# Hymba decoder block on one Trainium2 core: loading the output projection's operand two token tiles ahead

## The chip, the core and the metric

The kernel runs on one core of a Trainium2 chip. A core has TensorE (PE in the rows; its weight loads are PEld), VectorE (DVE), ScalarE (ACT), GpSimd (POOL) and SyncE (SP), each working through its own instructions in order; here every DMA is issued from SP's queue, also in order. The metric is the device time of one execution in microseconds (us): the median of the runs, lower is better. The kernel before takes 1448.87 us (median of 3 runs, 1448.34 to 1451.42).

## The reference

One layer of a hybrid decoder block, in float32: 1024 tokens and 16 meta tokens ahead of them, model width 1024.

```python
proj = rmsnorm(h, g_attn) @ w_in
# group A: 4 heads of differential attention; group B: 8 heads of stick-breaking attention
o_diff = _rmsnorm(o_diff, g_diff) * (1.0 - lam_init)
o_sb = _rmsnorm(o_sb, g_sb)
merged = jnp.concatenate([heads of o_diff, heads of o_sb], axis=-1)
h = h + merged @ w_out
h = h + (silu(gate) * up) @ w_down      # gate, up: causal convolution of rmsnorm(h, g_ffn) @ w_up
return _rmsnorm(h, g_final)[:, N_META:]
```

The change is in how the third line from the bottom, `merged @ w_out` and its addition to `h`, is fed.

## The kernel before

**The stages.** The program is written as strands (Python generators) that are advanced in turn, and a scheduler then places the instructions on each engine. Attention is done in eight units of 128 features: four heads of group A, then four pairs of group B. The score strand, the weigh strand and the norm strand carry attention. Everything else that PE can do meanwhile is the fill strand: the input projection of the next units, and, beside the last unit, the output projection. `attend` advances the fill strand so that the nanoseconds that it has yielded (`at["fill"]`) keep up with a share of the attention work done. A yield of a function instead of a number is a gate: the fill strand stays there until the function is true.

**The merged features.** For each unit the norm strand normalises a group of query tiles: PE transposes the norm factors (line 669), DVE multiplies (670), ACT and POOL split the result into a high and a low part, the tile `mc` (lines 672 and 673), and SP writes `mc` to `merged` in DRAM (674). The set `merged_at` tells which unit and tile has been written at that point of the program.

**The output projection.** It is done in three parts of the sum over units: OUT_A (units 0 to 2), OUT_B (3 to 5), OUT_C (6 and 7). Token tiles 5 to 8 are the late tiles, 3, 4, 0, 1, 2 the early ones (0 is the meta tile with two rows). The order of visits is OUT_A late, OUT_A early, OUT_B late, OUT_C late, OUT_B early, OUT_C early, in all 27 visits of a part and a tile. For each visit `load_merged` (line 702) fills a tile `mt` from `merged` by two DMAs (line 709; 192 KB each with three units, 128 KB with two), in OUT_A also the residual tile `acc` from `x` (line 711). Then `out_tile` (line 730) does two halves of 512 columns. Each half is 3 matmuls per unit into a bank `mm` of PSUM (line 743), 9 in OUT_A and OUT_B and 6 in OUT_C, and one DVE addition to `acc` (line 745). `out_meta` does the meta tile (lines 721 and 723).

**What sets the order around the change.** `out_part` (line 747) loads the next tile of the same part when it starts a tile, if that tile's features are in `merged_at`. `mt` has two buffers, so that load waits for the tile before the current one. The first tile of each part has no such load ahead of it: it is loaded where its turn comes. The very first load also has to wait until the input projection has read `xT` for the last time, because the pool of `mt` takes over that memory. SP's queue carries, between these loads, the writes of `merged` (line 674), the query swaps `qs` (522, 523), the weights (`raw`, line 684) and, later, the rows `y_rows` of the second norm (877).

After the output projection come the second norm, the feed-forward stages (lines 909 and 1045), and the down projection (1203, 1221).

Of the kernel before, what the change touches and what calls it, by code (L numbers as in the profile page):

```python
# [8 lines left out]
F32 = mybir.dt.float32  # L9
F32R = mybir.dt.float32r  # L10
# [3 lines left out]
ALU = mybir.AluOpType  # L14
# [3 lines left out]
P = 128  # L18
D = 1024
# [30 lines left out]
LATE_TILES = (5, 6, 7, 8)  # L50
EARLY_TILES = (3, 4, 0, 1, 2)
# [12 lines left out]
N_LATE = 12  # L64
AHEAD_OUT = 2
BEHIND = 2

# [28 lines left out]
def hybrid_block(ctx: ExitStack, tc: tile.TileContext, x, meta, g_attn, w_in, lq1, lk1, lq2, lk2,  # L96
                 g_diff, g_sb, w_out, g_ffn, w_up, conv_w, conv_b, w_down, g_final, out):
    nc = tc.nc
# [534 lines left out]
    merged_at = set()  # L633
# [53 lines left out]
    def load_split(src, tag, raw=None):  # L687
        raw = load_raw(src) if raw is None else raw
        bufs = 3 if tag == "wu" else 2
        hi = room[tag].tile([P, D], F32R, tag=tag + "h", name=tag + "h", bufs=bufs)  # L690
        lo = room[tag].tile([P, D], F32R, tag=tag + "l", name=tag + "l", bufs=bufs)
        nc.scalar.copy(hi, raw)
        nc.gpsimd.tensor_tensor(lo, raw, f(hi), op=ALU.subtract)
        return hi, lo
# [4 lines left out]
    def resid(t):  # L699
        return room["accm"][:2] if t == 0 else room["acc"][:, t - 1, :]  # L700

    def load_merged(t, us):
        c, n = q_span(t)
        mt = room["wd"].tile([P, 3, 2, P], F32R, tag="mt", name="mt", bufs=2)
        if t == 0:
# [8 lines left out]
    def out_meta(us, wo, mt):  # L714

        for h in range(2):
# [7 lines left out]
            if us is OUT_C:  # L724
                nc.scalar.copy(room["low"][:, hs], room["accm"][32:34, hs])
                nc.vector.tensor_tensor(resid(0)[:, hs], resid(0)[:, hs], room["low"][:, hs], op=ALU.add)
        if us is OUT_C:
# [7 lines left out]
    def out_tile(t, us, wo, mt):  # L735
# [10 lines left out]
        if us is OUT_C:  # L746
            square_sum(t)

    def out_part(us, wo, ts_):

        nxt = None
        for i, t in enumerate(ts_):
            if nxt is None:
                yield lambda: all((u, t) in merged_at for u in us)
                nxt = load_merged(t, us)
            mt, nxt = nxt, None
            if i + 1 < len(ts_) and all((u, ts_[i + 1]) in merged_at for u in us):
                nxt = load_merged(ts_[i + 1], us)
            yield from out_tile(t, us, wo, mt) if t else out_meta(us, wo, mt)

    def out_strand():
# [11 lines left out]
        room["accm"] = room["wd"].tile([34, D], F32, tag="wdh", name="accm", bufs=2)  # L773
        room["low"] = room["wd"].tile([2, D], F32, tag="wdl", name="low", bufs=2)
        nc.gpsimd.memset(room["accm"], 0.0)
# [415 lines left out]
    k = 0  # L1191
# [79 lines left out]
```

## Time and profile before

| What | us |
|---|---|
| median of 3 runs (lowest to highest) | 1448.87 (1448.34 to 1451.42) |
| the profiled execution | 1450.97 |
| its span, from the first to the last instruction | 1449.2 |
| PE busy in the span | 1359.0 (94%) |
| DVE, ACT, POOL busy | 969.8, 714.1, 745.1 |
| stretch with the output projection's matmuls | 548.5 to 734.0 |

The profiled execution is 2.1 us above the median. Its span leaves 1.8 us for what lies around the instructions. Matmuls are pipelined: a row's duration is longer than the distance from one start to the next, so a stretch is read by its starts, by the idle time in brackets, and by the granted clock, not by the durations alone. The granted clock is a fraction of 2.4 GHz: 1.00 is that level, and 0.51 over a stretch means that nearly all of it ran at the lower level of 1.2 GHz.

### The profile page before, as it was taken

What the parts mean: (1) busy time and instruction counts of PE and PEld (TensorE: products, weight loads), DVE (VectorE), ACT (ScalarE), POOL (GpSimd) and SP (SyncE); (2) the same over time, 40 slices, a digit from 0 to 9 for tenths busy, and PEclk for the clock granted to TensorE, in tenths of its full rate; (3) what the DMA queues carried; (4) which work ended last, traced back from release to release, by engine and by line L of the source; (5) the groups of instructions that cost most, each with busy time, mean ns of one, the idle gap of its engine ahead of it and who ended that gap; (6) DMA issues with size and microseconds to landing.
All of it is one profiled execution on the core that took longest, in us unless ns stands there. A gap on an engine that the chain in (4) does not pass through costs nothing.

```text
span 1449.2 us, 24692 instructions
## 1 busy us (share of the span) xinstructions
PE 1359.0 (94%) x9000; PEld 1259.0 (87%) x9000; DVE 969.8 (67%) x1816; ACT 714.1 (49%) x1406; POOL 745.1 (51%) x769
## 2 busy tenths in 40 slices
PE   5999989999998998898899999999999996999997
PEld 5989989998887796776689899999999995888886
DVE  8377868778676775874577545555556565977755
ACT  6255655666575664541344354445444453533322
POOL 5145444236665765662101376667666672965620
PEclk9999999999999998999999999999999998999999
DMA  5154454221211117333534222322323234966502
GB/s 211 51 179 154 143 166 139 59 67 38 60 44 50 46 46 207 92 90 93 143 109 162 92 70 95 109 93 78 100 96 110 94 104 163 335 206 199 179 15 102
DMA packets 93569, 166.35 MB, mean 115 GB/s; under 512 B 11628, under 2 KB 46060, under 8 KB 93448
## 3 DMA queue, kind: packets, MB, share of 16 engines
q1 hardware_dynamic: 93448, 164.78, 36.3%
q8 instruction: 71, 1.16, 0.3%
q14 instruction: 50, 0.41, 0.1%
HBM read 111.49 MB, written 44.85 MB: 108 GB/s over the span
## 4 chain that ended last, share of the span: by engine, by line
PE 68%; DVE 6%; DMA 4%; issue 3%; ACT 2%; POOL 2%; SPq 0%; DVEq 0%; POOLq 0%; ACTq 0%
PE x L1045 27%; PE ps_mm L296 7%; PE ps_x L1203 7%; PE ps_mm L743 5%; PE ps_y L1203 5%; PE ps_av L587 3%; DMA mt<-merged 3%; PE ps_tr L558 3%; DVE s L500 2%; PE ps_s L909 2%; PE ps_av L909 2%; PE ps_x L1221 2%; PE ps_y L1221 2%; PE ps_s L443 1%; PE ps_s L444 1%
## 5 line engine op out<-in xcount | busy, mean ns | idle before, releaser
L296 PE MATMUL ps_mm<-xT_hi,wh 128*128 128x342 f32 (+7 forms) x552 | 183.5, 333 | 4.8 <-DVE qz L306 3.5
L296 PE MATMUL ps_mm<-xT_lo,wh 128*128 128x342 f32 (+7 forms) x552 | 180.5, 328 | 0.2 <-DVE xT_lo L183 0.2
L296 PE MATMUL ps_mm<-xT_hi,wl 128*128 128x342 f32 (+7 forms) x552 | 179.9, 327 | 0.0
L587 PE MATMUL ps_av<-aT,v 128*128 128x256 f32 (+3 forms) x608 | 132.7, 309 | 3.1 <-POOL aT L565 2.6
L890 POOL TENSOR_TENSOR dl<-raw,dh 128x1024 fp32r<-128x1024 f32 (+1 forms) x43 | 82.1, 1910 | 90.1 <-ACT dh L889 88.5
L1045 PE MATMUL x<-yh,dl 128*128 128x258 f32 x608 | 124.2, 286 | 0.0
L1045 PE MATMUL x<-yl,dh 128*128 128x258 f32 x608 | 123.7, 285 | 0.0
L1045 PE MATMUL x<-yh,dh 128*128 128x258 f32 x608 | 123.7, 285 | 0.0
L296 PEld LDWEIGHTS ps_mm<-xT_hi,wh 128*128 128x128 f32 x552 | 106.1, 193 | 8.0 <-issue 2.6
L500 DVE TENSOR_TENSOR_SCAN s<-s 128x912 f32<-128x912 f32 (+6 forms) x72 | 99.3, 1383 | 20.6 <-POOL s L496 19.5
L558 PE MATMUL ps_tr<-ident,a 128*128 128x128 f32 (+1 forms) x540 | 94.2, 280 | 18.9 <-DVE aT L563 4.7
L1051 ACT COPY kept<-x 128x516 f32<-128x516 f32 x76 | 44.8, 589 | 133.6 <-PE x L1045 133.6
L1173 POOL TENSOR_TENSOR el<-down_raw,eh 128x512 fp32r<-128x512 f32 x53 | 91.3, 1752 | 35.9 <-ACT eh L1171 35.9
L587 PEld LDWEIGHTS ps_av<-aT,v 128*128 128x128 f32 (+2 forms) x608 | 97.1, 193 | 13.4 <-issue 4.4
L296 PEld LDWEIGHTS ps_mm<-xT_lo,wh 128*128 128x128 f32 x552 | 106.3, 193 | 1.1 <-DVE xT_lo L183 0.5
L501 POOL TENSOR_TENSOR a<-a,s 128x912 f32<-128x912 f32 (+3 forms) x64 | 82.1, 1286 | 47.5 <-DVE s L500 40.4
L296 PEld LDWEIGHTS ps_mm<-xT_hi,wl 128*128 128x128 f32 x552 | 106.0, 192 | 0.3
L570 DVE TENSOR_TENSOR aT<-ps_tr,aT 128x512 fp32r<-128x512 f32 (+3 forms) x132 | 76.7, 586 | 42.2 <-ACT aT L569 41.3
L1045 PEld LDWEIGHTS x<-yh,dh 128*128 128x128 f32 x608 | 95.3, 191 | 0.0
L1045 PEld LDWEIGHTS x<-yl,dh 128*128 128x128 f32 x608 | 95.1, 191 | 0.0
L1045 PEld LDWEIGHTS x<-yh,dl 128*128 128x128 f32 x608 | 95.0, 191 | 0.0
L569 ACT CAST aT<-ps_tr 128x512 fp32r<-128x512 f32 (+3 forms) x132 | 66.5, 510 | 56.1 <-PE ps_tr L558 53.2
(306 smaller groups left out, 4074.3 us busy)
## 6 DMA issues: line engine op xcount, KB each, us to landing
raw<-in_w_up SPq DMA_DIRECT2D x44, 512.0 KB, 3.6
down_raw<-blocks SPq DMA_DIRECT2D x63, 256.0 KB, 4.0
raw<-in_w_in SPq DMA_DIRECT2D x24, 512.0 KB, 3.6
blocks<-cg SPq DMA_DIRECT2D x45, 256.0 KB, 2.8
raw<-in_w_down SPq DMA_DIRECT2D x18, 512.0 KB, 3.6
down_sums<-raw SPq DMA_DIRECT2D x18, 512.0 KB, 3.2
down_raw<-down_sums SPq DMA_DIRECT2D x36, 256.0 KB, 4.6
down_raw<-in_w_down SPq DMA_DIRECT2D x27, 256.0 KB, 4.2
```

Source lines behind the costliest of these rows:

```text
L296: nc.tensor.matmul(ps[:, :w], a[:, kt * P : (kt + 1) * P], b[:, kt, c0 : c0 + w], start=(kt == 0 and i == 0), stop=(kt == KT - 1 and i == 2))
L500: nc.vector.tensor_tensor_scan(s[:n, rev], s[:n, rev], s[:n, rev], 1.0, op0=ALU.mult, op1=ALU.bypass)
L501: (nc.gpsimd if t else nc.vector).tensor_tensor(b[:n, :keys], b[:n, :keys], s[:n, 1 : keys + 1], op=ALU.mult)
L558: pe_last[0] = nc.tensor.transpose(ps[:kn, at : at + qn], a[:qn, kk0 : kk0 + kn], ident[:qn, :qn])
L569: nc.scalar.copy(aT[:kn, 0, f0:end], ps[:kn, f0:end])
L570: nc.vector.tensor_tensor(aT[:kn, 1, f0:end], ps[:kn, f0:end], f(aT)[:kn, 0, f0:end], op=ALU.subtract)
L587: pe_last[0] = nc.tensor.matmul(av[:, :w], v[:kn, kt, vi, :], aT[:kn, ai, j * w : (j + 1) * w], start=job["count"] == 0, stop=job["count"] ...
L743: nc.tensor.matmul(ps[:n], a, b[:, hs], start=(j == 0 and i == 0), stop=(j == len(wo) - 1 and i == 2))
L890: nc.gpsimd.tensor_tensor(lo[:, :w], src, f(hi)[:, :w], op=ALU.subtract)
L1045: nc.tensor.matmul(x[:, s], w[a][:, ks], y[b][:, kt, SUB * s : SUB * s + SUB + 2], start=start and kt == 0 and i == 0, stop=kt == KT // 2 ...
L1173: engine.tensor_tensor(lo[:, cs], raw[:, cs], f(hi)[:, cs], op=ALU.subtract)
L1203: nc.tensor.matmul(ps, a[:, P * t : P * (t + 1)], b[:, upper], start=begin and j == 0 and i == 0, stop=j == n - 1 and i == 2, skip_group_c ...
```

## The change

All 27 visits are listed in one table, `visits`, over the ends of the parts. When a visit starts, everything up to two visits further on is loaded, as far as its features are in `merged_at` at that point of the program; `mt` has three buffers. Where a visit's tile has not been loaded when its turn comes, the load is issued there and the fill strand yields LOAD_NS = 4000 ns, so that `attend` counts 4 us of fill work that isn't there and issues attention instead. The tile `low` for the meta row moves into two buffers of the pool tag `mc`, and the low part of one weight has one buffer instead of two.

```diff
--- before.py
+++ after.py
@@ -63,6 +63,7 @@
 S_AHEAD = 2
 N_LATE = 12
 AHEAD_OUT = 2
+LOAD_NS = 4000.0
 BEHIND = 2
 
 
@@ -686,9 +687,9 @@
 
     def load_split(src, tag, raw=None):
         raw = load_raw(src) if raw is None else raw
-        bufs = 3 if tag == "wu" else 2
-        hi = room[tag].tile([P, D], F32R, tag=tag + "h", name=tag + "h", bufs=bufs)
-        lo = room[tag].tile([P, D], F32R, tag=tag + "l", name=tag + "l", bufs=bufs)
+        bufs = {"wu": (3, 3), "wd": (2, 1)}.get(tag, (2, 2))
+        hi = room[tag].tile([P, D], F32R, tag=tag + "h", name=tag + "h", bufs=bufs[0])
+        lo = room[tag].tile([P, D], F32R, tag=tag + "l", name=tag + "l", bufs=bufs[1])
         nc.scalar.copy(hi, raw)
         nc.gpsimd.tensor_tensor(lo, raw, f(hi), op=ALU.subtract)
         return hi, lo
@@ -701,7 +702,7 @@
 
     def load_merged(t, us):
         c, n = q_span(t)
-        mt = room["wd"].tile([P, 3, 2, P], F32R, tag="mt", name="mt", bufs=2)
+        mt = room["wd"].tile([P, 3, 2, P], F32R, tag="mt", name="mt", bufs=3)
         if t == 0:
             nc.gpsimd.memset(f(mt)[:, : len(us), 0, :34], 0.0)
         for s in range(2):
@@ -722,8 +723,9 @@
                 yield 2 * 512 * COL
             nc.vector.tensor_tensor(room["accm"][:, hs], room["accm"][:, hs], ps[:34], op=ALU.add)
             if us is OUT_C:
-                nc.scalar.copy(room["low"][:, hs], room["accm"][32:34, hs])
-                nc.vector.tensor_tensor(resid(0)[:, hs], resid(0)[:, hs], room["low"][:, hs], op=ALU.add)
+                low = pn.tile([P, 2, 258], F32, tag="mc", name="low", bufs=2).rearrange("p a b -> p (a b)")[:2, :512]
+                nc.scalar.copy(low, room["accm"][32:34, hs])
+                nc.vector.tensor_tensor(resid(0)[:, hs], resid(0)[:, hs], low, op=ALU.add)
         if us is OUT_C:
             square_sum(0)
 
@@ -746,17 +748,34 @@
         if us is OUT_C:
             square_sum(t)
 
+    visits = [(us, t) for us, ts_ in ((OUT_A, LATE_TILES + EARLY_TILES), (OUT_B, LATE_TILES), (OUT_C, LATE_TILES),
+                                      (OUT_B, EARLY_TILES), (OUT_C, EARLY_TILES)) for t in ts_]
+    fetched = []
+
+    def there(k):
+        us, t = visits[k]
+        return all((u, t) in merged_at for u in us)
+
+    def fetch_until(k):
+
+        while len(fetched) <= min(k, len(visits) - 1) and there(len(fetched)):
+            us, t = visits[len(fetched)]
+            fetched.append(load_merged(t, us))
+
+    visit = [0]
+
     def out_part(us, wo, ts_):
 
-        nxt = None
-        for i, t in enumerate(ts_):
-            if nxt is None:
-                yield lambda: all((u, t) in merged_at for u in us)
-                nxt = load_merged(t, us)
-            mt, nxt = nxt, None
-            if i + 1 < len(ts_) and all((u, ts_[i + 1]) in merged_at for u in us):
-                nxt = load_merged(ts_[i + 1], us)
-            yield from out_tile(t, us, wo, mt) if t else out_meta(us, wo, mt)
+        for t in ts_:
+            k = visit[0]
+            visit[0] += 1
+            assert visits[k] == (us, t)
+            if k >= len(fetched):
+                yield lambda: there(k)
+                fetch_until(k)
+                yield LOAD_NS
+            fetch_until(k + 2)
+            yield from out_tile(t, us, wo, fetched[k]) if t else out_meta(us, wo, fetched[k])
 
     def out_strand():
         while len(w_ready) < AHEAD_OUT:
@@ -771,7 +790,6 @@
         nc.gpsimd.memset(room["ss"], 1.0)
         wa = w_ready + [load_split(None, "wd", raw)]
         room["accm"] = room["wd"].tile([34, D], F32, tag="wdh", name="accm", bufs=2)
-        room["low"] = room["wd"].tile([2, D], F32, tag="wdl", name="low", bufs=2)
         nc.gpsimd.memset(room["accm"], 0.0)
         yield from out_part(OUT_A, wa, LATE_TILES)
         yield lambda: done["weighed"] >= UNITS - 1
```

**The first load on PE.** PE's order behind the last matmuls on `xT`, where attention of the last units (lines 443, 444, 558, 587) meets the first output tile (line 743). Before:

```order
L444 MATMUL ps_s<-kz,qs 128x400
L443 MATMUL ps_s<-kz,qz 128x264
L444 MATMUL ps_s<-kz,qs 128x264
L558 MATMUL ps_tr<-ident,a 128x128 x4
L587 MATMUL ps_av<-aT,v 128x256
L743 MATMUL ps_mm<-wh,mt 128x512
L743 MATMUL ps_mm<-wl,mt 128x512
L743 MATMUL ps_mm<-wh,mt 128x512 x2
L587 MATMUL ps_av<-aT,v 128x256 x2
```

Now (all lines from 64 on count one higher, those of the projection two):

```order
L588 MATMUL ps_av<-aT,v 128x256 x4
L559 MATMUL ps_tr<-ident,a 16x128 x2
L588 MATMUL ps_av<-aT,v 128x256 x2
L559 MATMUL ps_tr<-ident,a 128x128 x4
L444 MATMUL ps_s<-kz,qz 128x264
L445 MATMUL ps_s<-kz,qs 128x264
L444 MATMUL ps_s<-kz,qz 2x16
L445 MATMUL ps_s<-kz,qs 2x16
L444 MATMUL ps_s<-kz,qz 128x256
L445 MATMUL ps_s<-kz,qs 128x256
L588 MATMUL ps_av<-aT,v 128x256 x4
L745 MATMUL ps_mm<-wh,mt 128x512
```

What stood behind the first matmuls on `mt` (line 587 x2 and on) now stands ahead of them: 27 more matmuls and transposes of attention lie between the last read of `xT` and the first use of `mt`.

**The first loads on SP.** SP's queue from the first load on; `mt_6911` and `mt_6915` (now `mt_6910`, `mt_7035`, `mt_7039`) are the tiles of the first visits. Before:

```order
L709 DMA mt_6911<-merged_83 128x3x128 x2
L711 DMA acc_6898<-in_x 128x1024
L709 DMA mt_6915<-merged_83 128x3x128 x2
L711 DMA acc_6898<-in_x 128x1024 x5
L684 DMA raw_7431<-in_w_out 128x1024
L711 DMA accm_6908<-in_meta 2x1024
L711 DMA acc_6898<-in_x 128x1024 x2
```

Now:

```order
L710 DMA mt_6910<-merged_83 128x3x128 x2
L712 DMA acc_6898<-in_x 128x1024
L710 DMA mt_7035<-merged_83 128x3x128 x2
L712 DMA acc_6898<-in_x 128x1024
L710 DMA mt_7039<-merged_83 128x3x128 x2
L712 DMA acc_6898<-in_x 128x1024 x4
L685 DMA raw_7528<-in_w_out 128x1024
```

A third tile's load goes out with the first two, ahead of four of the residual loads.

**From the norm to OUT_C on DVE.** The two rows `o<-o,gs,ps_tr` are the norm's products of unit 7 for the late tiles, from which the last features of OUT_C's late tiles come; `acc` rows are the half tiles of the output projection. Before (the last row is OUT_C's first half tile):

```order
L670 SCALAR_TENSOR_TENSOR o_7395<-o_7395,gs_78,ps_tr_7913 128x256
L670 SCALAR_TENSOR_TENSOR o_7554<-o_7554,gs_78,ps_tr_7921 128x256
L745 TENSOR_TENSOR acc_6898<-acc_6898,ps_mm_8197 128x512
L745 TENSOR_TENSOR acc_6898<-acc_6898,ps_mm_8208 128x512
L570 TENSOR_TENSOR aT_7980<-ps_tr_7979,aT_7980 128x128
L570 TENSOR_TENSOR aT_7988<-ps_tr_7987,aT_7988 128x512
L745 TENSOR_TENSOR acc_6898<-acc_6898,ps_mm_8219 128x512
L570 TENSOR_TENSOR aT_8001<-ps_tr_8000,aT_8001 128x384
L610 TENSOR_TENSOR o_8010<-ps_av_7985,tmp_8011 64x258
L563 TENSOR_TENSOR aT_8020<-ps_tr_8019,aT_8020 16x256
L745 TENSOR_TENSOR acc_6898<-acc_6898,ps_mm_8236 128x512
```

Now:

```order
L671 SCALAR_TENSOR_TENSOR o_7376<-o_7376,gs_78,ps_tr_7890 128x256
L671 SCALAR_TENSOR_TENSOR o_7509<-o_7509,gs_78,ps_tr_7898 128x256
L747 TENSOR_TENSOR acc_6898<-acc_6898,ps_mm_8163 128x512
L747 TENSOR_TENSOR acc_6898<-acc_6898,ps_mm_8174 128x512
L571 TENSOR_TENSOR aT_7957<-ps_tr_7956,aT_7957 128x128
L571 TENSOR_TENSOR aT_7968<-ps_tr_7967,aT_7968 128x512
L747 TENSOR_TENSOR acc_6898<-acc_6898,ps_mm_8188 128x512
L747 TENSOR_TENSOR acc_6898<-acc_6898,ps_mm_8199 128x512
L571 TENSOR_TENSOR aT_7981<-ps_tr_7980,aT_7981 128x384
L611 TENSOR_TENSOR o_7990<-ps_av_7962,tmp_7991 64x258
L564 TENSOR_TENSOR aT_7995<-ps_tr_7994,aT_7995 16x256
L747 TENSOR_TENSOR acc_6898<-acc_6898,ps_mm_8213 128x512
```

Behind the norm's rows three half tiles of OUT_B stood ahead of OUT_C; now there are six of them (the last of the six, and OUT_C's first behind it, follow the row that is last here).

## Rows read from the trace of the kernel before

**Rows 1.** The page: PE's busy tenths in 40 slices of 36.2 us; the last chain by line.

```profile
PE   5999989999998998898899999999999996999997
...
PE x L1045 27%; PE ps_mm L296 7%; PE ps_x L1203 7%; PE ps_mm L743 5%; PE ps_y L1203 5%; PE ps_av L587 3%; DMA mt<-merged 3%; PE ps_tr L558 3%; DVE s L500 2%; PE ps_s L909 2%; PE ps_av L909 2%; PE ps_x L1221 2%; PE ps_y L1221 2%; PE ps_s L443 1%; PE ps_s L444 1%
```

**Rows 2.** Waits, engine PE, 530 to 750 us: us in total, times, longest.

```profile
PE ps_mm L743 <- DMA mt<-merged: 15.2, 8, 4.6
```

**Rows 3.** Timeline, engine PE: start, us, instruction [idle before it <- what ended that].

```profile
548.49 0.80 PE L743 MATMUL ps_mm<-wh,mt 128*128 128x512 f32 x1 [4.57 <-DMA mt<-merged]
...
550.31 1.22 PE L743 MATMUL ps_mm<-wh,mt 128*128 128x512 f32 x2 [0.59 <-DMA mt<-merged]
...
667.46 0.79 PE L743 MATMUL ps_mm<-wh,mt 128*128 128x512 f32 x1 [3.94 <-DMA mt<-merged]
...
685.54 0.47 PE L743 MATMUL ps_mm<-wuh,mt 128*128 128x512 f32 x1 [1.42 <-DMA mt<-merged]
...
702.14 0.47 PE L743 MATMUL ps_mm<-wuh,mt 128*128 128x512 f32 x1 [3.64 <-DMA mt<-merged]
...
716.23 0.47 PE L743 MATMUL ps_mm<-wh,mt 128*128 128x512 f32 x1 [0.39 <-DMA mt<-merged]
```

**Rows 4.** Windows, engine PE: length, busy us (instructions), granted clock, DMA share, GB/s.

```profile
548.40:556.60 8.20, 7.52 (x28) 0.51 1.02 371
...
556.60:609.00 52.40, 48.49 (x273) 1.00 0.46 122
...
609.00:613.00 4.00, 2.40 (x13) 1.00 0.55 146
...
613.00:618.00 5.00, 4.73 (x20) 0.66 0.42 67
...
667.40:672.60 5.20, 5.14 (x12) 0.51 0.11 33
...
702.10:706.80 4.70, 4.66 (x13) 0.64 0.45 138
```

**Rows 5.** DMA issues, 541 to 734 us: number, size, median us from issue to landing.

```profile
mt<-merged SPq DMA_DIRECT2D x32, 192.0 KB, 5.1
...
mt<-merged SPq DMA_DIRECT2D x16, 128.0 KB, 3.6
```

**Rows 6.** Timeline, engine PE: inside a tile of OUT_C.

```profile
681.11 0.40 PE L743 MATMUL ps_mm<-wl,mt 128*128 128x512 f32 x1
...
681.80 0.39 PE L743 MATMUL ps_mm<-wl,mt 128*128 128x512 f32 x1
```

**Rows 7.** Timeline, SP's queue: start, time to the end of the row's last issue.

```profile
541.54 0.92 SPq L709 DMA_DIRECT2D mt<-merged  x2
...
657.47 1.21 SPq L674 DMA_DIRECT2D merged<-mc  x2
...
663.03 18.27 SPq L709 DMA_DIRECT2D mt<-merged  x9
```

**Rows 8.** Timeline, engine POOL, while PE waits for the first load.

```profile
543.52 2.35 POOL L261 TENSOR_TENSOR wl<-raw,wh 128x1024 fp32r<-128x1024 f32 x1
...
545.86 2.34 POOL L693 TENSOR_TENSOR wdl<-raw,wdh 128x1024 fp32r<-128x1024 f32 x1
```

**Rows 9.** Timeline, engine PE: attention matmuls right behind the first loads.

```profile
551.33 0.63 PE L587 MATMUL ps_av<-aT,v 128*128 128x256 f32 x2
...
554.10 0.63 PE L743 MATMUL ps_mm<-wl,mt 128*128 128x512 f32 x1
```

**Rows 10.** Timeline, engine PE: the norm's last transposes ahead of OUT_C's late part.

```profile
654.91 0.60 PE L669 MATMUL ps_tr<-ident,yb 128*128 128x128 f32 x4
```

**Rows 11.** Timeline, engine PE: attention's own waits.

```profile
609.03 0.66 PE L558 MATMUL ps_tr<-ident,a 128*128 128x128 f32 x4 [1.43 <-DVE aT L570]
...
612.96 0.44 PE L669 MATMUL ps_tr<-ident,yb 128*128 128x128 f32 x2 [1.57 <-ACT yb L660]
```

**Rows 12.** Windows, engine DVE: length, busy us (instructions), granted clock, DMA share, GB/s.

```profile
712.00:731.00 19.00, 16.71 (x35) 1.00 0.53 153
```

## What I expect, written before the changed kernel ran

> **What bounds the kernel now.** I read the page's slices and its last chain first, then PE's waits grouped by what ended them, then PE's timeline at the longest of those waits, and last the windows around them for the granted clock.
>
> The slices show PE at 8 or 9 tenths nearly everywhere [rows 1], and PE is busy for 1359.0 of 1449.2 us. What holds PE up passes to the end: after the output projection the slices stay at 9, and the last chain carries "DMA mt<-merged" as 3% of itself. So this stretch is paid for in PE's time and in PE's waits.
>
> The waits say how much: matmuls on `mt` stood idle for 15.2 us, 8 times, the longest 4.6 [rows 2]. The timeline places six of the eight [rows 3]. The very first tile waits 4.57 us and, for its second DMA, 0.59. The first tile of OUT_C waits 3.94, the first of OUT_B early 1.42, and at 702.14 a tile inside OUT_B early, the one behind the small meta tile, 3.64. The rest is short, as the 0.39 at 716.23.
>
> A wait costs a second time, by the granted clock. In the stretch behind the first it is 0.51, which is all but wholly the 1.2 GHz level, for 7.52 busy us; behind the wait at 667.46 also 0.51, for 5.14 busy us; behind the one at 702.14 0.64, for 4.66 busy us. Between them it is 1.00 [rows 4]. In each case PE had been idle for 3.6 us or more just before.
>
> **The change, part by part.** The sum is made against the profiled execution, 1450.97 us, and then carried to the median, 2.1 lower.
>
> *The waits after the first load.* They are 15.2 − 4.57 − 0.59 = 10.0 us, of which three make 3.94 + 1.42 + 3.64 = 9.0. A load lands 5.1 us after its issue with three units, 3.6 with two [rows 5]. Inside a tile, three matmuls go from 681.11 to 681.80 [rows 6], 0.23 us each. So a tile of OUT_A or OUT_B with 18 matmuls takes 4.1 us, one of OUT_C with 12 takes 2.8, both less than their loads. With two buffers a load is released one tile ahead, and at a part's start none goes ahead at all. With three buffers, over the ends, it is released two tiles ahead: 8.2 us against 5.1, 5.6 against 3.6, and at the tile behind the meta tile 4.1 for a whole tile and 2.8 for the meta tile's 12 matmuls, 6.9 against 5.1, where only the 2.8 stood before. So the three long waits go: 9.0. Of the last 1.0 in the short ones I take half, because around them DVE is busy for 16.71 of 19.00 us [rows 12] and would be late next. Together **9.5** (bounds 9.0 and 10.0).
>
> *The clock behind those waits.* At 1.00 the work behind 667.46 would take 5.14 × 0.51, which frees 2.5; that behind 702.14 4.66 × 0.64, which frees 1.7. Together **4.2** (bounds 0, if another wait keeps the clock low there, and 4.2).
>
> *The first load.* It is still issued where `xT` becomes free, at 541.54 [rows 7], and the matmuls on it still can't start before 548.5. What is new is that 27 matmuls and transposes of attention now stand ahead of the first use. Are they ready? Those that stood right behind the first loads ran from 551.33 to 554.10 [rows 9], 2.8 us at half clock, so 1.4 at full. The later ones depend on DVE and ACT; DVE had the whole wait to get ahead. I take 1.4 and another 0.6 for these, **2.0**; bounds 0 (nothing ready) and 5.2 (the whole wait covered). It is nearest to the row at 551.33, since these are the very instructions. The clock behind it I leave as it is: in 609 to 613 PE was busy for 2.40 of 4.00 us, and the stretch behind that ran at 0.66 [rows 4], so a wait that is half filled need not keep the clock.
>
> *What may come new.* The norm's last transposes for OUT_C's late tiles start at 654.91 [rows 10]; from there to the first use of those features at 667.46 it is 12.55 us, through DVE, POOL, SP's write at 657.47 and the load at 663.03 [rows 7]. That chain is not shorter now. Three half tiles of PE's work stood in it before; six stand there now, 3 × 2.05 = 6.1 us more, against a wait of 3.94: spare 2.2 us. POOL has the subtraction of a weight's low part in 2.35 us [rows 8], which may now stand ahead of this chain's subtraction and takes just that spare. The last part has a like chain with less between. Attention gives way meanwhile, and its own waits, as 1.43 for DVE and 1.57 for ACT [rows 11], may grow. I take **−2.0**, between 0 and −4 (one wait like that at 667.46).
>
> *What costs nothing.* The DMAs are the same in number (54 on `mt`), as are the matmuls. The issues take 0.46 us of SP each [rows 7] and move ahead of residual loads that are needed only by DVE, behind a tile's first half. `low` in a buffer of `mc` would have to wait for a write of `merged`; at the end of OUT_C these are done, else it would be DVE's additions that come late. The low part's second buffer held nothing but `low`, so that nothing waits for it now.
>
> Sum: 9.5 + 4.2 + 2.0 − 2.0 = **13.7**. 1450.97 − 13.7 = 1437.3 for the profiled execution, **1435.2** for the median.
>
> **The rivals.**
>
> *A. The third buffer gives nothing; only the starts of parts gain.* SP's queue is in order, and nine issues on `mt` are spread over 18.27 us from 663.03 on [rows 7], each held by the one before. If a load two tiles ahead stands behind one that is itself held, the tile behind the meta tile is as late as before. Then 3.94 + 1.42 + 2.5 + 2.0 − 2.0 = 7.9 is gained: 1441.0. Against it: the buffer it waits for is now released a whole tile earlier, and the held load in front of it with it. The Trainium skill (Trainium Kernel Development and Optimization, Best Practices) asks for double buffering so that DMA and compute overlap; by it two buffers would do, and this result would come. The trace speaks against it here: with two buffers a landing of 5.1 us stands against a tile of 4.1. Chance 0.14.
>
> *B. The clock stays up behind the first load too.* If the attention moved ahead fills the 4.57 us well, the 7.52 busy us behind it run at 1.00 and free 7.52 × 0.49 = 3.7: 13.7 + 3.7 = 17.4, so 1431.5. For it: the wait shrinks below 3 us, and 1.43 and 1.57 at 609 to 613 came in the middle of a stretch that itself ran at 1.00. Against it: the stretch right behind ran at 0.66. The Trainium skill (TensorE: Matmul & The Clock Gate, Part 1) says that the slow level is the default and that recent activity of PE lifts it; by it the clock is kept where the filler is dense, and our rows at 609 to 618 show what a thin one does. Chance 0.12.
>
> *C. The features come late all the same.* If SP's write of `merged` or POOL's split is moved behind held loads, OUT_C waits at the start of both of its parts, each 3.94 + 2.5 = 6.4. Then 13.7 − 12.9 = 0.8 is left: 1448.1. For it: the chain of 12.55 us has only 2.2 to spare. Against it: SP issues the write at 657.47 well before the loads at 663.03, and both parts would have to be hit. Chance 0.08.
>
> *D. Slower: attention loses its cover.* LOAD_NS holds the fill strand 4 us back at the first load and the filler that it saves is then spent earlier, so that where attention has to wait for DVE there is less of the output projection to put between. One such place, as at 609 to 618, costs 1.43 + 1.57 of idle and 4.73 × 0.34 = 1.6 of clock, 4.6 in all [rows 4, 11]. 13.7 / 4.6 is 3.0 places to break even; with four, 18.4 is lost against 13.7: 4.7 slower, 1453.6. For it: DVE is near its bound in parts of this stretch [rows 12]. Against it: the filler's sum is the same, and only what is idle in both cases is lost. Chance 0.08.
>
> **How the numbers follow.** The forecast has 0.58, A 0.14, B 0.12, C 0.08, D 0.08. The low end is B with half of what is left of the first wait, (5.2 − 2.0) / 2 = 1.6, gained, and the new waits at their better bound, 2.0: 1431.5 − 3.6 = 1428, rounded. The high end is A with nothing from the first load and the new waits at their worse bound: 1441.0 + 2.0 + 2.0 = 1445. C and D lie outside. A measurement of this kernel tells 0.2%, 2.9 us, from no change. Forecast, A and B are faster by more than that, 0.84; C is within it, 0.08; D is slower, 0.08.
>
> **What would show it.** Right: PE's waits on `mt` fall from 15.2 to about 3.7 in all, the first of them to about 3; none stands at OUT_C's two starts nor behind the meta tile, and the clock there is near 1.00. A shows as a wait of over 3 us behind the meta tile, B as a clock above 0.8 behind the first load, C as waits for `mt` at OUT_C with the write of `merged` just before, D as PE waiting for DVE or ACT in attention, in rows that are new. Wrong would be above all a gain of under 3 us with the waits on `mt` gone: then another engine was the bound behind them.

## The result

The changed kernel takes 1429.26 us (median of 4 runs, 1427.28 to 1431.79) against 1449.31 before (4 runs, 1448.34 to 1451.42): a ratio of 0.9864, 95% interval 0.9846 to 0.9882, 20 us less. The forecast was 1435.2 with a range of 1428 to 1445. The sign and the range hold; the gain is larger than the likeliest case, and rival B at 1431.5 came closest.

The page of the changed kernel: the slices of PE, the granted clock in tenths in the same slices, and the last chain by line.

```profile
PE   5999989999998998899999899999999996999997
...
PEclk9999999999999999999999999999999998999999
...
PE x L1063 27%; PE ps_x L1221 7%; PE ps_mm L297 7%; PE ps_y L1221 5%; PE ps_mm L745 5%; DVE s L501 3%; PE ps_av L588 2%; PE ps_tr L559 2%; PE ps_s L927 2%; PE ps_av L927 2%; PE ps_x L1239 2%; PE ps_y L1239 2%; PE ps_s L444 1%; PE ps_s L445 1%; PE ps_tr L180 1%
```

PE's slices differ from [rows 1] in three of the 40, each by a tenth, and its busy time is 1347.5 of 1425.9 us. "DMA mt<-merged", 3% of the chain before, no longer stands in this line.

The longest waits of PE, 530 to 735 us (us in total, times, longest), answering to [rows 2]:

```profile
PE ps_tr L670 <- ACT yb L661: 2.3, 2, 1.6
PE ps_tr L180 <- DVE yl L184: 2.0, 1, 2.0
PE ps_tr L559 <- DVE o L671: 1.9, 1, 1.9
PE ps_mm L745 <- DVE acc L747: 1.3, 1, 1.3
...
```

No wait for `mt` is left, of 15.2 us. What holds PE now are waits of attention, of the norms and of the output projection's own additions (`acc`) for DVE and ACT, none of them over 2 us.

In the kernel before, the last read of `xT` stood here, 7.1 us ahead of the first use of `mt` at 548.49 [rows 3]:

```profile
541.35 0.28 PE L296 MATMUL ps_mm<-xT_hi,wl 128*128 128x256 f32 x1
```

The timeline of PE in the changed kernel, from the last read of `xT` to the first use of `mt`, where 4.57 us of idle stood before:

```profile
537.78 0.28 PE L297 MATMUL ps_mm<-xT_hi,wl 128*128 128x256 f32 x1
...
540.51 0.51 PE L588 MATMUL ps_av<-aT,v 128*128 128x256 f32 x2 [0.18 <-ACT aT L570]
541.24 0.55 PE L559 MATMUL ps_tr<-ident,a 128*128 128x128 f32 x3 [0.22 <-DVE aT L571]
...
543.44 0.66 PE L559 MATMUL ps_tr<-ident,a 128*128 128x128 f32 x4 [0.42 <-DVE aT L571]
...
545.35 0.39 PE L444 MATMUL ps_s<-kz,qz 128*128 128x256 f32 x1 [0.97 <-ACT s L489]
...
546.16 0.39 PE L745 MATMUL ps_mm<-wh,mt 128*128 128x512 f32 x1
```

and the windows of PE around it, around three stalls of attention, and at the start of OUT_C and in OUT_B early (columns as in [rows 4]):

```profile
537.90:546.10 8.20, 6.26 (x46) 1.00 0.59 113
546.10:554.30 8.20, 7.51 (x48) 1.00 1.03 369
...
599.00:603.00 4.00, 2.04 (x11) 0.81 0.61 90
603.00:606.00 3.00, 2.74 (x9) 0.50 0.00 1
606.00:609.00 3.00, 3.00 (x10) 0.61 0.36 125
...
658.10:663.30 5.20, 5.20 (x24) 1.00 0.41 86
677.00:692.00 15.00, 15.00 (x72) 1.00 0.77 196
```

The stalls of attention in those windows:

```profile
599.06 0.44 PE L670 MATMUL ps_tr<-ident,yb 128*128 128x128 f32 x2 [1.61 <-ACT yb L661]
...
600.27 0.58 PE L670 MATMUL ps_tr<-ident,yb 2*128 2x2 f32 x3 [0.23 <-DVE aT L571]
...
603.26 1.33 PE L559 MATMUL ps_tr<-ident,a 128*128 128x128 f32 x5 [1.89 <-DVE o L671]
```

The attention that stood behind the first loads now runs in front of them. It waits itself, 0.18 + 0.22 + 0.42 + 0.97 = 1.79 us, but the load no longer holds PE when it is through: the first matmul on `mt` starts at 546.16 with no idle time. Over the wait and behind it the clock is 1.00, where 7.52 busy us had stood at 0.51 [rows 4]. The lower level shows at one place in the output projection. The 0.81 ahead of 603 and the 0.61 behind 606 put it from about 601.5 to about 608.3, so it began as the third of the three waits (1.61, 0.23 and 1.89 us) had just begun, at 601.4.

The two profiles differ by 23.3 us of span, 3.3 more than the medians. That part is no work of the change. PE's order is the same in both up to the last read of `xT`, but that read came at 541.35 before and at 537.78 now. Most of it arose around 200 us, in the same matmuls. Before:

```profile
175.00:215.00 40.00, 35.71 (x232) 0.91 0.50 150
```

After:

```profile
174.00:211.00 37.00, 32.93 (x231) 1.00 0.54 160
```

The same work took 3 us longer, at a mean clock of 0.91. So below, idle time and clock are summed only from the last read of `xT` to a common point some 240 to 260 us on, from which the same number of matmuls remains. "Idle" sums the brackets of PE's timeline; "clock" sums busy time times (1 − granted clock) over windows of 2 us.

| kernel | median, us | ratio to before (95%) | stretch | idle on `mt` | other idle | clock |
|---|---|---|---|---|---|---|
| before | 1449.31 | 1 | 258.7 | 15.2 | 9.0 | 11.2 |
| the change | 1429.26 | 0.9864 (0.9846 to 0.9882) | 239.7 | 0 | 12.5 | 4.3 |
| no filler | 1442.71 | 0.9971 (0.9960 to 0.9983) | 250.9 | 9.2 | 11.9 | 8.4 |
| filler only | 1436.91 | 0.9925 (0.9911 to 0.9938) | 248.5 | 2.9 (see below) | 14.8 | 5.8 |
| two buffers | 1437.03 | 0.9929 (0.9915 to 0.9944) | 245.5 | 4.4 (see below) | 12.3 | 4.2 |
| one visit ahead | 1428.58 | 0.9880 (0.9864 to 0.9896) | 239.2 | 0 | 12.3 | 4.2 |
| no visit ahead | 1429.95 | 0.9884 (0.9868 to 0.9901) | 240.1 | 0 | 12.6 | 4.2 |
| idle matmuls for filler | 1437.44 | 0.9931 (0.9915 to 0.9947) | 245.7 | 4.0 | 10.3 | 6.2 |
| filler at the 2nd visit | 1440.26 | 0.9959 (0.9943 to 0.9974) | 250.0 | 5.0 | 13.4 | 8.8 |
| filler at the 10th visit | 1441.41 | 0.9953 (0.9935 to 0.9972) | 252.7 | 9.2 | 12.3 | 10.1 |
| LOAD_NS 2000 | 1441.85 | 0.9966 (0.9953 to 0.9979) | 252.3 | 5.5 | 13.4 | 11.0 |
| LOAD_NS 3000 | 1440.80 | 0.9954 (0.9937 to 0.9971) | 249.7 | 3.0 | 15.8 | 7.9 |
| LOAD_NS 6000 | 1432.23 | 0.9903 (0.9885 to 0.9921) | 239.7 | 0 | 12.0 | 5.0 |
| LOAD_NS 8000 | 1434.26 | 0.9914 (0.9893 to 0.9934) | 242.6 | 0.6 | 10.8 | 10.1 |

The stretch of the change is 19.0 us shorter: 15.2 less idle on `mt`, 6.9 less lost to the clock, 3.5 more of other idle time, and 0.4 of rest. That is the 20 us of the medians, within their interval. Each kernel's ratio is to runs of before on its own chip (medians of before there: 1446.64 for no filler, filler only, two buffers and one visit ahead; 1447.32 for no visit ahead, idle matmuls, the 10th visit and 8000; 1447.53 for the 2nd visit, 2000 and 3000; 1446.65 for 6000). One visit ahead and no visit ahead are equal to the change within the intervals. Stretch, idle and clock come from one trace of each kernel. Outside the stretch the traced spans lie between 1186 and 1193 us, and two kernels with the same order on PE and SP (filler only and two buffers, see below) differ by 3 us in the stretch: a difference of that size there shows nothing.

### The profile page after: what moved, and what is told of

Its sections match the earlier page's. It is cut to its first block, busy times and chain, and to the rows that moved or that the text cites. A ratio compares the mean times of both kernels' runs of the same rounds, so it can differ in the third digit from the quotient of the medians.

```text
span 1425.9 us, 24695 instructions
## 1 busy us (share of the span) xinstructions
PE 1347.5 (95%) x9000; PEld 1251.1 (88%) x9000; DVE 967.8 (68%) x1816; ACT 714.9 (50%) x1406; POOL 749.2 (53%) x769
## 4 chain that ended last, share of the span: by engine, by line
PE 66%; DVE 9%; issue 4%; ACT 3%; POOL 2%; DMA 1%; SPq 0%; DVEq 0%; POOLq 0%; ACTq 0%
PE x L1063 27%; PE ps_x L1221 7%; PE ps_mm L297 7%; PE ps_y L1221 5%; PE ps_mm L745 5%; DVE s L501 3%; PE ps_av L588 2%; PE ps_tr L559 2%; PE ps_s L927 2%; PE ps_av L927 2%; PE ps_x L1239 2%; PE ps_y L1239 2%; PE ps_s L444 1%; PE ps_s L445 1%; PE ps_tr L180 1%
```

## The experiments

The theory was that two things work apart: loads ahead in a third buffer take away the waits inside the output projection, and the filler takes away the first load's wait with its clock. Its rivals were that one of them does all, that two buffers are enough, and that the place of a load in the program counts.

**Loads ahead, no filler.**

```diff
-LOAD_NS = 4000.0
+LOAD_NS = 0.0
```

> The changed kernel with LOAD_NS = 0: loads two ahead over the ends in three buffers, but no attention pulled in front of the first use. My theory: the first load's part of the gain is idle time plus clock, 4.57 + 0.59 + 3.7 of clock behind it, less some 2 to 3 us of new attention waits that the filler brought. So this kernel is 6 to 7 us slower than the changed one, near 1436 (13 faster than before); PE waits some 5 us for mt at the first load alone, and the granted clock behind it is near 0.5. Rival (the early loads did it all, the filler moved nothing that counts): within 2 us of the changed kernel, 1428 to 1431. Rival (the filler is the larger part): 1441 or more.

It took 1442.71, a ratio of 0.9971: 4 us faster than before and 13 slower than the change, twice the 6 to 7 of the theory, and what the second rival had said (the filler is the larger part). Timeline of PE: the first load's wait is back, as expected; the second row wasn't expected.

```profile
544.94 0.79 PE L745 MATMUL ps_mm<-wh,mt 128*128 128x512 f32 x1 [4.50 <-DMA mt<-merged]
...
546.95 1.22 PE L745 MATMUL ps_mm<-wh,mt 128*128 128x512 f32 x2 [0.79 <-DMA mt<-merged]
...
665.83 0.51 PE L745 MATMUL ps_mm<-wh,mt 128*128 128x512 f32 x1 [3.92 <-DMA mt<-merged]
```

SP's queue in this kernel, at OUT_C's features:

```profile
655.85 1.21 SPq L675 DMA_DIRECT2D merged<-mc  x2
661.33 10.25 SPq L710 DMA_DIRECT2D mt<-merged  x8
```

The wait at OUT_C's start stays, 3.92 us against 3.94 [rows 3], though this kernel asks for loads two visits ahead over the part's end. It isn't issued before the write of the last features has landed: the write at 655.85, the loads from 661.33 (in the changed kernel such a write takes 5.4 us to landing, median of 6). From the norm's last transposes to the first use it is 12.54 us, as the 12.55 before [rows 7, 10], with 27 matmuls on `mt` between them, counted in the timeline. In the change 54 stand there, and the chain of 16.21 us has no wait at its end. There the write starts at 644.21 and the load behind it at 650.89, 7.3 us ahead of its use at 658.18, where 4.5 us lie between here. So the filler, 100 us earlier, is what brings the norm ahead of OUT_C. The windows behind the two waits show the clock at 0.65 and 0.67:

```profile
544.80:553.00 8.20, 7.27 (x33) 0.65 1.01 345
665.70:670.90 5.20, 5.08 (x15) 0.67 0.28 81
```

**Filler only, on the kernel before.**

```diff
                 nxt = load_merged(t, us)
+                if us is OUT_A and i == 0 and ts_ is LATE_TILES:
+                    yield 4000.0
```

> The kernel before with one thing added: 4000 ns counted as fill work after the first load, so attention is put there; two buffers and no load over the ends of parts, as before. My theory: 6 to 7 us faster than before, near 1442.5; the waits for mt at the first load gone, the three long ones at 667, 686 and 702 still there with their low clock. Rival (the later waits grow by what the first lost, since the fill strand runs behind): within 2 us of before, 1447 to 1451. The two halves of the change add up to its 20 us if they don't meet.

It took 1436.91, 9.7 us faster than before (0.9925, 0.9911 to 0.9938): more than the 6 to 7 of the theory, and far from the rival. The waits of PE and two of its rows:

```profile
PE ps_mm L743 <- DVE hn L169: 3.5, 2, 2.0
PE ps_mm L743 <- DMA mt<-merged: 2.4, 3, 1.1
```

```profile
675.84 0.47 PE L743 MATMUL ps_mm<-wuh,mt 128*128 128x512 f32 x1 [1.47 <-DVE hn L169]
...
690.84 0.47 PE L743 MATMUL ps_mm<-wuh,mt 128*128 128x512 f32 x1 [2.00 <-DVE hn L169]
```

There is no wait at OUT_C's start, with two buffers and no load ahead over a part's end. Two waits remain at OUT_B early, at its first tile and behind the meta tile. The view puts both down to `hn` on DVE, but SP's queue shows the load of the first one:

```profile
670.51 0.89 SPq L709 DMA_DIRECT2D mt<-merged  x2
```

Its issue starts at 670.51, and 5.1 us to landing [rows 5] lead to 675.6, next to the start of that tile at 675.84. The second stands where 702.14 stood; that it waits for its load is argued from that place. They are of the kind that [rows 3] show at 685.54 and 702.14, and the 3.5 us under `hn` belong by this to the idle time on `mt`.

**Two buffers, one visit ahead, over the ends; and three buffers, one visit ahead.**

```diff
-        mt = room["wd"].tile([P, 3, 2, P], F32R, tag="mt", name="mt", bufs=3)
+        mt = room["wd"].tile([P, 3, 2, P], F32R, tag="mt", name="mt", bufs=2)
...
-            fetch_until(k + 2)
+            fetch_until(k + 1)
```

> The changed kernel with two buffers for mt and each visit loading one visit further on, still over the ends of parts and with the filler. Theory (the third buffer counts, a landing of 5.1 us against a tile of 4.1): the wait behind the meta tile stays, about 3.6 us with 1.7 of clock, and 0.5 to 1 us at other tiles, so 5 to 8 us slower than the changed kernel, 1434 to 1437. Rival (two buffers are enough once the ends are bridged): within 2 us of the changed kernel.

The second of the two kernels has the second hunk alone:

> The changed kernel with its three buffers, but each visit asks for one visit further on instead of two. Theory: what releases a load is the buffer, which is that of the tile three visits back in both; SP's queue runs ahead of PE, so that being later in the program's order costs nothing: within 2 us of the changed kernel, no wait for mt over 1 us. Rival (the place in SP's queue counts): as with two buffers, 1434 to 1437.

With two buffers 1437.03, with three 1428.58: 8.4 us apart, with intervals that don't meet. The direction is the theory's; the size is just past its 5 to 8. With two buffers the wait behind the meta tile stays, shorter than the 3.6 that the theory gave it:

```profile
674.34 0.47 PE L745 MATMUL ps_mm<-wuh,mt 128*128 128x512 f32 x1 [1.47 <-DVE hn L170]
...
689.31 0.47 PE L745 MATMUL ps_mm<-wuh,mt 128*128 128x512 f32 x1 [2.53 <-DMA mt<-merged]
```

The wait of 1.47 is that of OUT_B's first early tile again, with its load issued at 669.02, 5.3 us before; it adds to the 4.4 of the table. With three buffers no wait for `mt` is left. In the traces the two kernels are 6.3 us apart in the stretch, 4.4 of them idle time, and the clock costs both the same: with two buffers it is low behind the meta tile, from 690.3 to 693.7, with three as long behind a wait of the second norm, from 725.3 on. The scheduler also orders PE otherwise with three buffers, in 333 places from 689 us on, so the 8.4 us are those of the buffer with the order that it brings.

By the medians the two-buffer kernel is equal to the filler alone, and the traces say why: by name and shape, PE's 9000 matmuls and transposes and SP's 548 issues stand in the same order in both. Bridging the parts' ends moved no instruction, so these two are one schedule run twice.

The expectation for the filler had said that the two halves of the change add up if they don't meet. By the medians on their common chip they don't add up: 9.7 (filler only) and 3.9 (no filler) make 13.6, against 18.1 for one visit ahead. By the traced stretches, 10.2 and 7.8 make 18.0, against 19.0 for the change. Which of the two holds stays open.

**Three buffers and the filler, nothing asked for ahead.**

```diff
                 fetch_until(k)
-                yield LOAD_NS
-            fetch_until(k + 2)
+                yield LOAD_NS if k == 0 else 0.0
```

> The changed kernel with its three buffers and its filler, but no load is asked for ahead at all: each visit's load is written where its turn comes. Theory (after one visit ahead gave the same as two): SP runs through its queue ahead of PE and only the buffer holds a load, so that the place of the load in the program does nothing: within 2 us of the changed kernel, 1427 to 1431, no wait for mt over 1 us. Rival (loads written late come late): waits for mt of 3 to 5 us at several tiles, 1440 or more.

1429.95, and no wait for `mt`: the same as the change. The table `visits` with its two tiles ahead, which gave the change its name, does nothing to the time. But the theory's reason isn't tested by this. PE's order is the same in the change, with one visit ahead and with none, and of SP's 548 issues only two stand elsewhere with one visit ahead, and four with none (a weight's load against the residual's, and `g_ffn` against a load of `mt`). So wherever the program writes the loads, they come out at nearly the same places of SP's queue, and there mostly the buffer holds them: SP's issues of `mt` between 540 and 720 us wait 14 times, 49.5 us in all, for the matmuls of line 745 that read the buffer before, and in the change 14 times, 48.2 us. What a load would lose that really stood later in the queue, these kernels don't show.

**Matmuls that nobody reads, in place of the filler.** This kernel computes 18 matmuls more, on the weights `wh` and without use for the output.

```diff
-LOAD_NS = 4000.0
+LOAD_NS = 0.0
...
                 fetch_until(k)
+                ps = bank("mm")
+                for _ in range(18):
+                    nc.tensor.matmul(ps, wo[0][0][:, :P], wo[0][0][:, :512], start=True, stop=True)
                 yield LOAD_NS
```

> The kernel without filler (LOAD_NS = 0) with 18 matmuls of 512 columns, on weights already there and with a result that nobody reads, beside the first load; 12 matmuls of attention slip in front with them. Theory (the wait is paid a second time by the clock, and work of any kind keeps it up): the time up to the first use stays as it is, the granted clock behind it is 0.9 or more instead of near 0.5, which frees 3.7, and the 12 moved matmuls free about 1: 4 to 5 us faster than that kernel without them (1442.7), 1437.5 to 1438.5. The wait for mt at the start of OUT_C stays. Rival (the clock behind the first load is low for another reason): within 2 us of 1442.7.

1437.44, where the theory said 1437.5 to 1438.5. PE's rows and windows:

```profile
540.98 0.28 PE L297 MATMUL ps_mm<-xT_hi,wl 128*128 128x256 f32 x1
...
545.52 2.33 PE L778 MATMUL ps_mm<-wh 128*128 128x512 f32 x9
...
549.19 0.39 PE L745 MATMUL ps_mm<-wh,mt 128*128 128x512 f32 x1
...
662.74 0.79 PE L745 MATMUL ps_mm<-wh,mt 128*128 128x512 f32 x1 [3.76 <-DMA mt<-merged]
```

```profile
549.10:557.30 8.20, 8.00 (x51) 1.00 1.04 367
662.70:667.90 5.20, 5.16 (x19) 0.69 0.23 68
```

The first matmul on `mt` starts 8.2 us behind the last read of `xT` at 540.98, as in the change (8.4), and the clock behind it is 1.00 instead of 0.65. That is 7.27 × 0.35 = 2.5 of the 5.2 us by which the stretch is shorter, less than the 3.7 of the expectation, since the level without these matmuls was 0.65 there and not 0.51; the rest is attention that was moved into the gap or waits less later. The wait at OUT_C, where nothing fills, stays at 3.76 with 0.69 behind it. By the ratios the kernel is 0.4% faster than without these matmuls (0.9931 against 0.9971, intervals apart). So a stretch about as long as the wait before, filled with work that is of no use, ended without the lower clock: matmuls that nobody reads kept it up here, together with the attention that slipped in. The Trainium skill (TensorE: Matmul & The Clock Gate, Part 1) says that recent activity of PE lifts the clock; the trace agrees, 1.00 against 0.65.

**The filler elsewhere.** Two kernels put it not at the first load but ahead of a later visit, the tenth (OUT_B's first late tile) and the second.

```diff
-                yield LOAD_NS
+                yield 0.0
+            if k == 9:
+                yield LOAD_NS
             fetch_until(k + 2)
```

> The changed kernel with its 4000 ns of counted fill work not at the first load but ahead of OUT_B's first late tile, 95 us later. Theory (the filler has a second effect: it moves the norm of unit 7 ahead of the output projection, and so brings OUT_C's features in time): the first load's wait of 4.5 + 0.8 comes back with a clock near 0.5 behind it, the wait of 3.9 at OUT_C's start is gone with its 2.5 of clock; about 6 us faster than without filler (1442.7), 1435 to 1438. Rival (the wait at OUT_C hangs on the first load's delay, or on loads ahead): the wait at OUT_C stays, 1441 to 1444.

1441.41, outside the theory's 1435 to 1438. It told nothing of the question: 27 matmuls stood between norm and OUT_C as without filler, and PE's order differs from that kernel's only between 639 and 651 us, in 39 places. That the fill strand was behind its share there and made up for the 4000 ns at once is likely, but only argued. The second kernel has `k == 1`:

> The changed kernel with its 4000 ns of counted fill work put ahead of the second visit (OUT_A, token tile 6) instead of the first; the order up to the first use of mt is as without filler, and 54 matmuls on mt stand between the norm of unit 7 and OUT_C's start, as in the changed kernel, not 27. (The filler ahead of OUT_B's late tiles had moved nothing: the fill strand stood behind its share there.) Theory (the filler has two effects, and the second is the norm's lead on OUT_C): the first load's wait of 4.5 + 0.8 and a clock near 0.5 stay, the wait of 3.9 at OUT_C's start and its 2.5 of clock go: 1435 to 1438, about 6 us faster than without filler (1442.7). Rival (the wait at OUT_C follows from the first load's delay): wait at OUT_C stays, 1441 to 1444.

1440.26, the mechanism right and the total wrong. PE's rows and windows:

```profile
545.50 0.80 PE L745 MATMUL ps_mm<-wh,mt 128*128 128x512 f32 x1 [4.73 <-DMA mt<-merged]
...
567.62 0.58 PE L588 MATMUL ps_av<-aT,v 128*128 128x258 f32 x1 [1.50 <-DVE aT L571]
570.03 1.12 PE L670 MATMUL ps_tr<-ident,yb 128*128 128x128 f32 x4 [1.83 <-ACT yb L661]
```

```profile
545.40:553.60 8.20, 7.88 (x37) 0.68 1.04 350
669.00:674.20 5.20, 5.20 (x23) 1.00 0.41 84
```

The first load's wait and its low clock are there, and OUT_C starts without a wait at a clock of 1.00, with 54 matmuls in front of it. So the second effect is the filler's own and doesn't hang on the first load. But of the 6 us only 2.4 are left (ratios 0.9971 and 0.9959, the intervals overlap): attention, pulled ahead where PE had enough to do, waits 1.50 for `aT` and 1.83 for `yb`, waits that the kernel without filler doesn't have at these places.

**The size of the filler.** Four kernels change LOAD_NS alone.

> The changed kernel with LOAD_NS = 2000: 25 matmuls of attention between the last read of xT and the first use of mt instead of 45. Theory: the wait at the first load is cut by a third to a half, 2 to 3 us are left, the clock behind it stays up for a part; OUT_C's features come in part earlier. Between none (1442.7) and 4000 (1428.6), 1433 to 1438. Rival (2000 already keeps the clock and the order): within 2 us of the changed kernel.

> The changed kernel with LOAD_NS = 3000: 31 matmuls between the last read of xT and the first use of mt, 45 on mt between the norm and OUT_C's start. Theory: about 1 us of wait is left at the first load and the clock is kept; the chain to OUT_C has 9 matmuls, 2 us, less than with 4000 and still no wait; attention's own waits near 600 become shorter by what is used up less: 1426 to 1431, same as the changed kernel. Rival (the best is at the full 4000): 2 to 5 us slower, 1431 to 1434.

> The changed kernel with LOAD_NS = 6000: more than 45 matmuls of attention between the last read of xT and the first use of mt, 63 on mt between the norm of unit 7 and OUT_C's start. Theory (after 0, 2000 and 3000 gave 1442.7, 1441.9 and 1440.8, 4000 1428.6 and 8000 1434.3: what counts is that the first load's wait and OUT_C's wait are both gone and that attention is not stripped of cover): no wait for mt at either place, attention's waits between those of 4000 and 8000: 1428 to 1433. Rival (it is the order of attention that the number happens to give, and no rule): anywhere between 1426 and 1441, with waits at other places than in either neighbour.

> The changed kernel with LOAD_NS = 8000. Theory: the first load is covered by 4000 already, so nothing is left to gain there; 4 us more of attention are used up early, and where attention waits for DVE or ACT (1.6 and 1.9 us at 599 and 603) less of the output projection stands between: 0 to 3 us slower than the changed kernel, 1428 to 1432. Rival (the more filler the better): 1425 or less.

1441.85, 1440.80, 1432.23 and 1434.26, with 1442.71 at 0 and 1429.26 at 4000. The expectations for 2000 and 3000 failed: no share of the gain comes with a share of the filler. That for 6000 held; that for 8000 failed too (1434.26 against 1428 to 1432). With 2000 the waits are shorter, but PE's rows show both still there:

```profile
545.41 0.80 PE L745 MATMUL ps_mm<-wh,mt 128*128 128x512 f32 x1 [3.20 <-DMA mt<-merged]
...
666.49 0.59 PE L745 MATMUL ps_mm<-wh,mt 128*128 128x512 f32 x1 [2.03 <-DMA mt<-merged]
```

The wait at OUT_C follows the number of matmuls on `mt` between the norm's last transposes and its start: 3.92 us with 27 (no filler), 2.03 with 36 (2000), none with 45 (3000) or 54 (4000). With 3000 the first wait is down to 2.02 as well, yet attention has a long wait of its own:

```profile
548.10 0.50 PE L745 MATMUL ps_mm<-wh,mt 128*128 128x512 f32 x1 [2.02 <-DMA mt<-merged]
...
610.70 1.09 PE L559 MATMUL ps_tr<-ident,a 128*128 128x128 f32 x4 [4.57 <-DVE aT L571]
```

DVE's timeline shows what it waited behind:

```profile
603.96 5.93 DVE L501 TENSOR_TENSOR_SCAN s<-s 128x656 f32<-128x656 f32 x1
...
609.87 0.68 DVE L571 TENSOR_TENSOR aT<-ps_tr,aT 128x512 fp32r<-128x512 f32 x1
```

This scan takes 5.93 us, where its like takes 1.59 in the change (at 589.9). Two operations of POOL, of 2.38 and 2.02 us, run beside it; whether they stretch it no run here settles. So a part of what 3000 lacks is one slow instruction in the order that the number happened to give, as the rival in the expectation for 6000 says, and not the size of the filler.

With 6000 and 8000 no wait for `mt` is left at either place; PE waits elsewhere instead. In the kernel with 8000, 10.1 us go to the clock, 6.9 of them from 550 to 564, behind the first of these two waits. There PE was busy throughout and the clock stayed at the lower level:

```profile
549.80 1.15 PE L559 MATMUL ps_tr<-ident,a 128*128 128x128 f32 x5 [1.81 <-DVE v L336]
...
596.95 0.50 PE L745 MATMUL ps_mm<-wh,mt 128*128 128x512 f32 x1 [2.71 <-DVE acc L747]
```

```profile
550.00:564.00 14.00, 14.00 (x51) 0.51 1.02 310
```

4000 is the best of the six; the interval of 6000 (0.9885 to 0.9921) overlaps that of one visit ahead (0.9864 to 0.9896). No kernel beat the change.

## Why the prediction was right, and where not

- **Waits after the first load, 9.5:** 10.0 went, the size was right. The cause was half wrong. The sentence "With three buffers, over the ends, it is released two tiles ahead" was to explain all three long waits. The third buffer takes away those at OUT_B early (8.4 us by the medians, two buffers against three); asking ahead takes away nothing (1429.95 without it, in nearly the same order of SP's queue). And the 3.94 at OUT_C wasn't a late load but late features. The chain of 12.55 us was in the text, with its 3 half tiles against 6, but only as a risk; it was the cause, as 3.92 with 27 matmuls, 2.03 with 36 and none with 54 show. So 3.94 of idle and 2.5 of clock, 6.4 of the 13.7 forecast, came by another road than the one given for them, through the filler; that the sum holds them is luck.
- **Clock behind those waits, 4.2:** right in size, with 2.5 of it by that other road. In the changed kernel 658 to 663 and 677 to 692 run at 1.00.
- **First load, 2.0:** mis-sized. The whole 5.16 went; the attention in front of it waited 1.79, so 3.4 net. "The later ones depend on DVE and ACT", taken at 0.6, was too wary.
- **"The clock behind it I leave as it is":** this is the step that failed. It stayed at 1.00, worth 3.7. The row that I argued from, 2.40 busy of 4.00 followed by 0.66, was a stretch with two waits of 1.43 and 1.57 (the prediction's "idle for 3.6 us or more" ahead of each lower stretch leaves this one out); here 6.26 of 8.20 were busy and the longest wait was 0.97. Rival B had this right, and its 3.7 is what the forecast lacked.
- **New waits, −2.0:** measured 3.5 more of other idle, 1.79 of it at the first load, the rest above all the 1.89 at 603. The clock cost 2.6 us in the output projection around there, against 4.73 × 0.34 = 1.6 at 613 before, 1.0 more. The 3.5 lie within the bounds of 0 and 4, with the clock's 1.0 just past them, in a place that was named under D.
- **Rivals.** A fell: the wait behind the meta tile is gone, and it is gone by the third buffer; B came nearest, and its sign, a clock above 0.8 behind the first load, is there. The sign named for the forecast, some 3.7 us of waits on `mt` left, is not: none is left. The double buffering that the Trainium skill (Trainium Kernel Development and Optimization, Best Practices) asks for is 8.4 us short of three buffers here, as the landing of 5.1 against 4.1 us per tile had said. C fell in the changed kernel, but its late features remain, at one of the two starts, when the filler is taken out. D's mechanism, new waits of attention, showed with the filler at the second visit, where it took back a part of the gain; with 3000 and 8000 new waits came too, beside a slow scan and a long stretch at the lower clock. No kernel became slower than before.

In sums: 10.0 + 4.2 + 5.2 + 3.7 − 3.5 − 1.0 = 18.6, against 19.0 in the stretch.

## What to carry to other kernels

Find out for a wait on a load whether the buffer, the queue or the data was late: a load that goes out right behind the landing of the write that it reads was not helped here by a third buffer or by asking earlier (3.92 us against 3.94), but by putting the producer ahead of other work (none with 54 matmuls between). Before crediting a move in the program, compare the order that comes out on the engines: asking two visits ahead left 544 of SP's 548 issues where they were without it. And a gap on PE is worth filling with work that is ready, since the clock behind it cost 3.7 us beside a gap of 4.57 here, but only as far as the work is ready: of six sizes of the filler, two that differ by 1000 ns lie 11.5 us apart.

## What was not expected of the hardware

The same instructions in the same order took 3 us more around 200 us in one execution than in the other, with idle time of 4.3 and 4.1 us there: it is spread otherwise. In the profile of before, waits of 1.66 and 1.73 us for `aT` end at 186.9 and 189.2, and from 190 to 194 the clock is 0.50; in the other the one wait there is 1.27 and the clock stays at 1.00. So two waits below 2 us, close together, went with a lower clock that cost some 3 us, and whether they fell so close differed between these two executions.

The changed kernel shows both in one trace: 1.79 us idle in four pieces over 8.2 us left the clock at 1.00; with 1.61, 0.23 and 1.89 within 6 us it was at 0.50 from about 601.5, when the third wait had just begun, to about 608.3. And with a filler of 8000 the lower level lasted from 550 to 564 behind a wait of 1.81 us, though PE was busy for all 14.00 us: the length of the wait alone doesn't tell the price.
